# Band and stick-breaking attention: weights of B as differences, late division in A, and two more tiles turned by VectorE

## The chip, the cores and the metric

The kernel runs on one core of one Trainium2 chip. The metric is the device time of one execution in microseconds (us); the median of several executions is compared. PE is TensorE, DVE VectorE, ACT ScalarE, POOL GpSimd and SP the engine from whose queue all transfers (DMAs) of this kernel are issued. Each engine works off its instructions in the order in which they were written into its queue.

## What is computed

One layer of a hybrid encoder, for 1024 prompt frames and for 32 sample frames with a cache of 512. Width 1024; two groups of 8 heads of 64, A and B. All in float32.

```python
qa, ka, va, ga, qb, kb, vb, gb = split(rmsnorm(h, g_pre) @ w_in)

def band_attention(q, k, v, q_pos, k_pos, bias_table):          # A
    s = q @ k.T * 64**-0.5 + bias_table[clip(k_pos - q_pos, -128, 128) + 128]
    ok = same chunk of 64 frames, or one of the 8 chunks before
    return softmax(where(ok, s, -1e30)) @ v

def stick_breaking(q, k, v, q_pos, k_pos):                      # B
    z = q @ k.T * 64**-0.5
    causal = k_pos < q_pos
    log_1m = where(causal, log_sigmoid(-z), 0.0)
    after = cumsum(log_1m, reverse=True) - log_1m               # over later keys
    w = where(causal, exp(log_sigmoid(z) + after), 0.0)
    return w @ v

y = concat(oA * silu(ga), oB * silu(gb)) @ w_out
h = h + rmsnorm(y, g_post)
h = h + sigmoid(h @ w_ple_gate) * (p @ w_ple)
```

In words, a weight of B is sigmoid(z) of its key times the product of sigmoid(-z) over all later keys up to the query.

## The kernel before

**Stages.** The input is normalised and turned so that the model width lies on the partitions. A projection of 128 columns of `w_in` (`col_steps`) is 3 chunks of 352 frames with 24 products each. The eight pairs of heads come in the order A0, B0, A1, B1, A2, B2, A3, B3; while the attention of one pair runs, the projections k, q and v of the next are computed, and beside the last pair the eight gate projections (`mm_gA`, `mm_gB`). Then follow the output projection (`o`), the second norm and the last gate (`g`), with a Strassen-like scheme of seven products.

**Products in parts.** A float32 operand is split into an upper half `hi` (rounded to fp32r, a copy) and a lower half `lo` (the difference), and products are summed over the halves. So every operand that PE reads costs a copy, mostly on ACT, and a subtraction, on DVE or POOL.

**Attention of a head** (`attention`). Eight tiles i of 128 queries. A tile of A reads the key blocks from max(0, i - 4) to i, a tile of B the blocks from 0 to i, so tiles of B grow from 1 to 8 blocks (36 a head), those of A to 5 (30 a head).

- `scores(i)`: PE puts the scores into one or two PSUM banks (`SA`, `SB`; tag S, three banks). For A, DVE adds the bias (`biasA`) and takes the running maximum in one operation (`tensor_tensor_reduce`, in the profile CUSTOM_DVE_ANT_0), negates the maximum, ACT takes the exponential with the sum, DVE the reciprocal, POOL scales. For B, DVE masks the diagonal block, ACT takes sigmoid(-z) into `w0` and sigmoid(z) into `w1`, DVE runs the product from the last key backwards (`tensor_tensor_scan`, shifted by one column), and POOL multiplies the two.
- `weights_t(i)`: the weights are turned so that keys lie on the partitions. In general PE does it block by block (`ptwA`, `ptwB`), ACT takes the upper half from PSUM into `wTh`, DVE the lower half into `wTl`. Tiles in `ROUND` go another way: DVE turns 32x32 squares from `w1` into `w0` (STREAM_TRANSPOSE), one DMA stores the result (`swapA`), four load it back into `w1` with the blocks in their places, and the halves are taken from there. Before the change these are tiles 4 and 6 of A.
- `values(g)`: for each half g of the head's queries one accumulation of `wT` with the values (`PVA`, `PVB`) and a sum of two row groups, stored in `o_dr`.

Tiles 4 and 6 have 5 blocks each in A, 5 and 7 in B.

**Rooms.** `w0` and `w1` of a tile lie in two rings of columns (`Arena`: `om` with 3076, `be` with 3384 columns), `wTh` and `wTl` in rings of 33 blocks. A room in a ring is given out in order, and taken again only when its last reader is done. A head of B takes 13 blocks for its first half and 29 for its second; one of A 13 and 20.

**Order.** All instructions are first recorded (`Recorder`) with their dependences. A planner (`order`) then runs a list schedule with a cost for each operation, a margin for landing transfers and a rule for the access path that DVE and POOL share, and the kernel is written in the order that comes out. On PE, attention has precedence over the projections wherever it is ready. Any change to an operation's engine or size therefore changes the order of much else.

**Gates.** A gate chunk loads its part of the head output (`og`), takes the sigmoid on ACT, and multiplies on DVE and POOL. All recorded operations have the one source line 450 in the profile; tiles are told apart by name.

## Time and profile before

| | |
|---|---|
| median of 3 runs | 806.25 us |
| the runs | 804.82, 806.25, 810.35 us |
| span of the profiled execution (first to last instruction) | 802.6 us |
| its busy time: PE, DVE, ACT, POOL | 792.0, 565.7, 539.5, 469.5 us |
| moved by DMA | 146.32 MB, 182 GB/s |

The execution that was profiled has no time of its own beside its span; the median stands 3.65 us above the span. A line of a group gives engine, operation, what is written and read by the program's names, partitions x elements, the number of instructions, then busy time, mean ns of one, idle time of the engine just before them and what ended it. A group without a single shape mixes several ("+3 forms"). A busy time of PE counts overlapping records once. In a timeline the columns are start, duration, engine, operation; in the chain of waits start and length of a piece of the chain. A row of the stages gives the stretch, its length, and for PE, the weight loads (PEld), DVE, ACT and POOL the busy time and number of instructions, then granted clock, DMA share and GB/s. SPq is the queue from which transfers are issued.

### The profile page before, as it was taken

The page shows a single profiled execution, that of the slowest core. Times are in us where ns is not written, and L with a number is a line of the kernel's source. Part 1 is how long each engine was busy: PE and PEld are TensorE (multiplying, and loading weights), DVE is VectorE, ACT ScalarE, POOL GpSimd, SP SyncE. Part 2 cuts the span into 40 slices and gives each one's busy share as a digit, 9 for nine tenths or more (in the row PEclk, how much of TensorE's full clock was granted, in tenths as well). Part 3 has the DMA queues.
Part 4 walks back from the last instruction along what each step waited for, and adds up shares of the span by engine and source line. Part 5 has one row for each costly group of instructions (what it writes and reads, how often), then busy time and mean ns, then how long its engine had stood idle before and what let it go on. Part 6 is the DMA issues. An engine that isn't in the chain of part 4 may idle for free.

```text
span 802.6 us, 14554 instructions
## 1 busy us (share of the span) xinstructions
PE 792.0 (99%) x4734; PEld 731.4 (91%) x4734; DVE 565.7 (70%) x1129; ACT 539.5 (67%) x1163; POOL 469.5 (58%) x554
## 2 busy tenths in 40 slices
PE   9999999999999999999999999999999999999997
PEld 7899999999999999999999899999998877888786
DVE  7627878777787888776787586854554786587655
ACT  6636787786586777776787577644437868876741
POOL 6625867795686866635473265554553448599613
PEclk9999999999999999999999999999999999999999
DMA  9419986538876565833325656344389957769634
GB/s 293 135 46 285 236 230 186 153 112 254 220 229 198 145 184 158 208 103 102 92 60 141 146 158 205 99 149 138 105 277 300 288 174 242 236 197 345 215 117 131
DMA packets 147390, 146.32 MB, mean 182 GB/s; under 512 B 37409, under 2 KB 109257, under 8 KB 147314
## 3 DMA queue, kind: packets, MB, share of 16 engines
q1 hardware_dynamic: 147314, 145.39, 61.3%
q8 instruction: 38, 0.62, 0.3%
q14 instruction: 38, 0.31, 0.1%
HBM read 90.78 MB, written 46.16 MB: 171 GB/s over the span
## 4 chain that ended last, share of the span: by engine, by line
PE 89%; DVE 3%; DMA 2%; POOL 2%; ACT 1%; issue 1%; SPq 1%; POOLq 0%; DVEq 0%; ACTq 0%
PE mm_gB L450 6%; PE mm_gA L450 6%; PE mm_kB L450 6%; PE mm_qB L450 6%; PE mm_qA L450 5%; PE mm_kA L450 5%; PE mm_vB L450 4%; PE PVB L450 4%; PE mm_vA L450 4%; PE SB L450 4%; PE ptwB L450 4%; PE SA L450 3%; PE PVA L450 3%; PE g0P L450 2%; PE g1P L450 2%; PE o1P L450 2%
## 5 line engine op out<-in xcount | busy, mean ns | idle before, releaser
L450 POOL TENSOR_TENSOR be<-be,om 128x512 f32<-128x512 f32 (+8 forms) x66 | 82.9, 1260 | 77.8 <-DVE om L450 43.9
L450 DVE TENSOR_TENSOR_SCAN om<-om,SB 128x384 f32<-128x384 f32 (+5 forms) x96 | 92.6, 968 | 21.9 <-ACT be L450 11.7
L450 POOL TENSOR_SCALAR be<-be,statA 128x640 f32<-128x640 f32 (+3 forms) x64 | 44.4, 698 | 44.4 <-DVE statA L450 35.8
L450 DVE TENSOR_TENSOR wTl<-ptwB,wTh 128x512 fp32r<-128x512 f32 (+3 forms) x96 | 50.8, 546 | 13.8 <-ACT wTh L450 12.4
L450 ACT ACTIVATE om<-SB 128x384 f32<-128x384 f32 (+5 forms) x96 | 47.4, 499 | 19.0 <-DVE SB L450 14.2
L450 ACT CAST wTh<-ptwB 128x512 fp32r<-128x512 f32 (+3 forms) x96 | 44.6, 483 | 14.5 <-PE ptwB L450 10.5
L450 ACT ACTIVATE be<-om,statA 128x640 f32<-128x640 f32 (+3 forms) x64 | 44.6, 698 | 11.2 <-DVE statA L450 9.6
L450 ACT ACTIVATE be<-SB 128x384 f32<-128x384 f32 (+5 forms) x96 | 46.8, 498 | 6.8 <-DVE om L450 6.3
L450 PE MATMUL ptwB<-ident,be 128*128 128x128 f32 x288 | 44.0, 273 | 0.1
L450 PEld LDWEIGHTS ptwB<-ident,be 128*128 128x128 f32 x288 | 34.9, 140 | 2.2 <-PE mm_vA L450 0.4
L450 DVE CUSTOM_DVE_ANT_0 om<-SA,biasA 128x320 f32<-128x320 f32 (+2 forms) x64 | 30.7, 480 | 5.3 <-PE SA L450 4.9
L450 PE MATMUL SB<-kdB,LB 128*128 128x384 f32 (+5 forms) x96 | 34.0, 357 | 0.3 <-DVE om L450 0.3
L450 ACT CAST wTh<-ptwA 128x512 fp32r<-128x512 f32 (+2 forms) x64 | 26.0, 429 | 12.0 <-PE ptwA L450 11.4
L450 DVE TENSOR_TENSOR wTl<-ptwA,wTh 128x512 fp32r<-128x512 f32 (+2 forms) x64 | 29.7, 482 | 4.9 <-ACT wTh L450 4.0
L450 PE MATMUL SB<-klB,LB 128*128 128x384 f32 (+5 forms) x96 | 32.9, 347 | 0.0
L450 PE MATMUL SA<-kdA,LA 128*128 128x320 f32 (+2 forms) x96 | 30.0, 319 | 1.1 <-DVE LA L450 0.8
L450 PE MATMUL SA<-klA,LA 128*128 128x320 f32 (+2 forms) x96 | 29.8, 319 | 0.0
L450 POOL TENSOR_TENSOR gB<-gB,gB 128x256 f32<-128x256 f32 x32 | 26.6, 848 | 0.7 <-DMA gB<-in_w_ple_gate_dram 0.4
L450 PE MATMUL ptwA<-ident,be 128*128 128x128 f32 x160 | 26.5, 274 | 0.0
L450 DVE TENSOR_TENSOR SB<-SB,maskb 128x128 f32<-128x128 f32 x64 | 18.0, 292 | 9.9 <-PE SB L450 8.0
L450 POOL TENSOR_TENSOR oB<-oB,oB 128x256 f32<-128x256 f32 x32 | 23.6, 754 | 1.4 <-DMA oB<-in_w_out_dram 1.3
L450 POOL TENSOR_TENSOR h<-h,x 128x512 f32<-128x512 f32 (+1 forms) x18 | 23.0, 1295 | 0.8 <-DVE h L450 0.8
(706 smaller groups left out, 2668.3 us busy)
## 6 DMA issues: line engine op xcount, KB each, us to landing
swapA<-om SPq DMA_DIRECT2D x16, 320.0 KB, 3.5
be<-swapA SPq DMA_DIRECT2D x64, 80.0 KB, 2.9
oB<-in_w_out_dram SPq DMA_DIRECT2D x16, 256.0 KB, 3.9
sum_dro<-oB SPq DMA_DIRECT2D x16, 256.0 KB, 2.9
gB<-in_w_ple_gate_dram SPq DMA_DIRECT2D x16, 256.0 KB, 3.7
sum_drg<-gB SPq DMA_DIRECT2D x16, 256.0 KB, 3.2
x<-in_x_prompt_dram SPq DMA_DIRECT2D x16, 256.0 KB, 4.1
h_dr<-h SPq DMA_DIRECT2D x8, 512.0 KB, 3.6
```

The costliest lines, as they stand in the source:

```text
L450: getattr(getattr(tc.nc, o.what[0]), o.what[1])(*args, **kw)
```

## The change

- **Differences for B.** The scan is no longer shifted: it runs in place over sigmoid(-z), so that `w0` holds the running products P, with a 1 behind the last key. The weight is P of the next key less P of its own, since sigmoid(z) = 1 - sigmoid(-z). The second sigmoid goes, and POOL's product becomes a subtraction. The sample heads of B keep the old way.
- **Late division for A.** The exponentials stay unscaled. Their sums are kept for the whole head; behind the last tile they are inverted together, turned by PE and stored in `rs_dr`. A gate chunk of A loads them spread over 64 partitions, and POOL multiplies once more. The sample columns of `rs_dr` are filled with ones.
- **Signs.** Queries of A, the bias and the mask are negated, so the reduction takes a minimum and the exponential a scale of -1; the negation of the maximum goes.
- **Turned tiles.** Tiles 4 and 6 of B are turned by DVE squares and DMAs too. The lower halves of all such tiles are subtracted by POOL in place of DVE.
- **Rooms.** The ring `be` shrinks to 3328 columns; `og` moves from the tag `bias` (2 deep) to `stg` (3 deep).

```diff
@@ -28,7 +28,7 @@
 
 
 
-ROUND = {"A": ((4,),(6,)), "B": ()}
+ROUND = {"A": ((4,),(6,)), "B": ((4,),(6,))}
 LAG_T = 2
 LAG_V = 2
 SPACE_S = 0.1
@@ -477,6 +477,7 @@
         return Buf(shape, F32, name=name, real=dram.tile(shape, F32, tag=name, name=name))
 
     o_dr = [scratch([P, T], f"o_dr{n}") for n in range(8)]
+    rs_dr = scratch([8, T], "rs_dr")
     og_dr = scratch([8, P, T], "og_dr")
     h1_dr = scratch([T, D], "h1_dr")
     sum_dr = {w: scratch([4, 4, P, 512], f"sum_dr{w}") for w in "og"}
@@ -511,7 +512,7 @@
     at0 = rec.pool(ctx, tc, name="at0", bufs=1)
     at = rec.pool(at_stack, tc, name="at", bufs=1)
     opnd = [at0, at]
-    ring0, ring1 = Arena(rec, at, "om", 3076), Arena(rec, at, "be", 3384)
+    ring0, ring1 = Arena(rec, at, "om", 3076), Arena(rec, at, "be", 3328)
     ringh, ringl = (Arena(rec, at, x, 33 * P, F32R) for x in ("wTh", "wTl"))
 
     def rstd_of(ms, name, n):
@@ -524,6 +525,11 @@
 
 
     NAMES = ["qA", "kA", "vA", "gA", "qB", "kB", "vB", "gB"]
+
+    def fixed_columns():
+        x = small.tile([8, NS], F32, tag="fixed", name="fixed")
+        nc.gpsimd.memset(x, 1.0)
+        dma(rs_dr[:, SEQ:T], x)
 
     raws, loaded = {}, {}
 
@@ -609,8 +615,8 @@
         dma(rb, rel_bias[0])
         R = ring1.tile([8, 768], "R")
         nc.gpsimd.memset(R, 0.0)
-        nc.vector.tensor_scalar(R[:, 256:768], R[:, 256:768], rb[:, 0:1], None, ALU.add)
-        nc.vector.tensor_copy(R[:, 0:256], rb[:, 0:256][:, ::-1])
+        nc.vector.tensor_scalar(R[:, 256:768], R[:, 256:768], rb[:, 0:1], None, ALU.subtract)
+        nc.vector.tensor_scalar(R[:, 0:256], rb[:, 0:256][:, ::-1], -1.0, None, ALU.mult)
         dma(r_dr, R)
 
     def bias_src(h, rows, first, cols):
@@ -728,8 +734,12 @@
             acc = box["acc"]
             cs = slice(c * CH, (c + 1) * CH)
             if k == "g" and part == 0:
-                box["og"] = at2.tile([P, CH], F32, tag="bias", name=f"og{kind}{p}_{c}", bufs=2)
-                dma(box["og"], o_dr[n][:, cs])
+                box["og"] = at2.tile([P, 2, CH], F32, tag="stg", name=f"og{kind}{p}_{c}", bufs=3)
+                dma(box["og"][:, 0], o_dr[n][:, cs])
+                if ab == "A":
+                    for h in range(2):
+                        row = rs_dr.real[2 * p + h:2 * p + h + 1, cs]
+                        dma(box["og"][h * HD:(h + 1) * HD, 1], Raw(rs_dr, bass.AP(tensor=row.tensor, offset=row.offset, ap=[[0, HD], [1, CH]])))
             W = loaded[j]
             for x in range(part * 24 // PARTS, (part + 1) * 24 // PARTS):
                 q, k8 = x // KD, x % KD
@@ -742,10 +752,12 @@
                 sg = at2.tile([P, 512], F32, tag="sg", name=f"sg{kind}{p}_{c}", bufs=3)[:, 0:CH]
                 nc.scalar.activation(sg, acc, AF.Sigmoid)
                 nc.vector.tensor_tensor(sg, acc, sg, ALU.mult)
-                nc.gpsimd.tensor_tensor(sg, sg, box["og"], ALU.mult)
+                nc.gpsimd.tensor_tensor(sg, sg, box["og"][:, 0], ALU.mult)
+                if ab == "A":
+                    nc.gpsimd.tensor_tensor(sg, sg, box["og"][:, 1], ALU.mult)
                 dma(og_dr[n, :, cs], sg)
             elif k == "q":
-                nc.scalar.activation(box["st"][:, cs], acc, AF.Copy, scale=SCALE)
+                nc.scalar.activation(box["st"][:, cs], acc, AF.Copy, scale=-SCALE if ab == "A" else SCALE)
             else:
                 nc.scalar.copy(box["st"][:, cs], acc)
 
@@ -785,9 +797,10 @@
             if ab == "A":
                 bias = at2.tile([P, 640], F32, tag="bias", name=f"bias{nm}", bufs=2)
                 dma(bias, bias_src(2 * p + h, P, 0, 640))
-                nc.gpsimd.memset(bias[0:HD, 0:HD], NEG)
-                nc.gpsimd.memset(bias[HD:P, 576:640], NEG)
+                nc.gpsimd.memset(bias[0:HD, 0:HD], -NEG)
+                nc.gpsimd.memset(bias[HD:P, 576:640], -NEG)
                 box["bias"] = bias
+                box["sums"] = small.tile([P, 8], F32, tag="sums", name=f"sums{nm}", bufs=2)
 
         def lo_block(i):
             return max(0, i - 4) if ab == "A" else 0
@@ -832,23 +845,26 @@
                 nc.gpsimd.memset(w0[:, n:n + 1], 1.0)
                 for a, b, s in pieces:
                     nc.scalar.activation(w0[:, a:b], s, AF.Sigmoid, scale=-1.0)
-                for a, b, s in pieces:
-                    nc.scalar.activation(w1[:, a:b], s, AF.Sigmoid)
                 for a, b, s in reversed(pieces):
-                    rev = w0[:, a + 1:b + 1][:, ::-1]
-                    nc.vector.tensor_tensor_scan(rev, rev, s, 1.0 if b == n else w0[:, b + 1:b + 2], ALU.mult, ALU.bypass)
-                nc.gpsimd.tensor_tensor(w1[:, 0:n], w1[:, 0:n], w0[:, 1:n + 1], ALU.mult)
+                    rev = w0[:, a:b][:, ::-1]
+                    nc.vector.tensor_tensor_scan(rev, rev, s, w0[:, b:b + 1], ALU.mult, ALU.bypass)
+                nc.gpsimd.tensor_tensor(w1[:, 0:n], w0[:, 1:n + 1], w0[:, 0:n], ALU.subtract)
             else:
                 m = small.tile([P, 4], F32, tag="stat", name=f"stat{nm}_{i}", bufs=6)
+                sums = box["sums"]
                 for j, (a, b, s) in enumerate(pieces):
                     nc.vector.tensor_tensor_reduce(
                         w0[:, a:b], s, box["bias"][:, n - b:n - a][:, ::-1], 1.0,
-                        -3e38 if j == 0 else m[:, j - 1:j], ALU.add, ALU.max, m[:, j:j + 1])
+                        3e38 if j == 0 else m[:, j - 1:j], ALU.add, ALU.min, m[:, j:j + 1])
                 last = len(pieces) - 1
-                nc.vector.tensor_scalar(m[:, 2:3], m[:, last:last + 1], -1.0, None, ALU.mult)
-                nc.scalar.activation(w1[:, 0:n], w0[:, 0:n], AF.Exp, bias=m[:, 2:3], accum_out=m[:, 3:4])
-                nc.vector.reciprocal(m[:, 3:4], m[:, 3:4])
-                nc.gpsimd.tensor_scalar(w1[:, 0:n], w1[:, 0:n], m[:, 3:4], 1.0, ALU.mult, ALU.mult)
+                nc.scalar.activation(w1[:, 0:n], w0[:, 0:n], AF.Exp, bias=m[:, last:last + 1], scale=-1.0, accum_out=sums[:, i:i + 1])
+                if i == 7:
+                    nc.vector.reciprocal(sums, sums)
+                    pt = psum("T", f"pts{nm}")
+                    nc.tensor.transpose(pt[0:8, 0:P], sums, ident)
+                    row = at.tile([P, 4 * P], F32, tag="ot", name=f"sumrow{nm}", bufs=2)[0:8, 0:P]
+                    nc.scalar.copy(row, pt[0:8, 0:P])
+                    dma(rs_dr[2 * p + h, 0:SEQ].rearrange("(i q) -> i q", q=P), row)
             state[i] = w0, w1
 
         wT = {}
@@ -890,7 +906,7 @@
                     src = turned[:, :, first[x]:first[x] + cost(x), :]
                     hi, lo = (y.rearrange("p (b g q) -> p g b q", g=4, q=32) for y in (hi, lo))
                     nc.scalar.copy(hi, src)
-                    nc.vector.tensor_tensor(lo, src, f(hi), ALU.subtract)
+                    nc.gpsimd.tensor_tensor(lo, src, f(hi), ALU.subtract)
                 done_with.clear()
                 return
             for b in range(0, n, 4):
...
@@ -1382,6 +1397,7 @@
         dma(*x)
         rec.behind()
     bias_rows()
+    fixed_columns()
     for h in range(4):
         dma(masks[h * NS:(h + 1) * NS, :], maskb[0:NS, 0:NS])
     for j in range(3):
```

In the sample heads of A (left out) the same three signs change.

More of the change, by code (lines that the diff above doesn't have):

```diff
@@ L1017, in scores @@
                         w0[:, a0:b0], s, bx["bias"][:, NK - b0:NK - a0][:, ::-1], 1.0,
-                        -3e38 if j == 0 else m[:, 0:1], ALU.add, ALU.max, m[:, j:j + 1])
-                nc.vector.tensor_scalar(m[:, 2:3], m[:, 1:2], -1.0, None, ALU.mult)
-                nc.scalar.activation(w1[:, 0:NK], w0[:, 0:NK], AF.Exp, bias=m[:, 2:3], accum_out=m[:, 3:4])
+                        3e38 if j == 0 else m[:, 0:1], ALU.add, ALU.min, m[:, j:j + 1])
+                nc.scalar.activation(w1[:, 0:NK], w0[:, 0:NK], AF.Exp, bias=m[:, 1:2], scale=-1.0, accum_out=m[:, 3:4])
                 nc.vector.reciprocal(m[:, 3:4], m[:, 3:4])
```

## The prediction

> **What bounds the kernel now.** I read the page first (parts 1, 2, 4, 5), then the groups by shape, the chain of waits in one stretch, the stages, and the timelines of a B head.
>
> ```profile
> PE 792.0 (99%) x4734; PEld 731.4 (91%) x4734; DVE 565.7 (70%) x1129; ACT 539.5 (67%) x1163; POOL 469.5 (58%) x554
> PEclk9999999999999999999999999999999999999999
> PE 89%; DVE 3%; DMA 2%; POOL 2%; ACT 1%; issue 1%; SPq 1%; POOLq 0%; DVEq 0%; ACTq 0%
> L450 POOL TENSOR_SCALAR be<-be,statA 128x640 f32<-128x640 f32 (+3 forms) x64 | 44.4, 698 | 44.4 <-DVE statA L450 35.8
> L450 ACT CAST wTh<-ptwB 128x512 fp32r<-128x512 f32 (+3 forms) x96 | 44.6, 483 | 14.5 <-PE ptwB L450 10.5
> L450 ACT ACTIVATE be<-SB 128x384 f32<-128x384 f32 (+5 forms) x96 | 46.8, 498 | 6.8 <-DVE om L450 6.3
> L450 PE MATMUL ptwB<-ident,be 128*128 128x128 f32 x288 | 44.0, 273 | 0.1
> ```
>
> PE is busy in 792.0 of 802.6 us at full granted clock and carries 89% of the chain. So work taken from PE shortens the run, provided PE still always has something ready; work on DVE, ACT and POOL counts only through the waits it makes. The 288 turnings of B's weights are PE work that the change cuts by a third: blocks of tiles 4 and 6 are 5 + 7 = 12 of 36 a head, over 8 heads 96. A busy PE is pipelined, so the worth of one turning is read from the chain, where pieces don't overlap:
>
> ```profile
> 300.63 0.77 PE ptwB L450 x7
> 306.81 0.87 PE ptwB L450 x8
> ```
>
> Seven take 0.77 us, eight 0.87: 0.110 us each, not the 273 ns of the record.
>
> **The change part by part.** *PE.* 96 x 0.110 = 10.6 us go. The sums of A's late division add one turning a head of 8, at most 0.110 each (it is a smaller one): 0.9 us come. Net -9.7 us. Nothing else on PE changes.
>
> *DVE.* The rows:
>
> ```profile
> L450 DVE TENSOR_TENSOR wTl<-ptwB,wTh 128x512 fp32r<-128x512 f32 x48 | 32.4, 681 | 12.1 <-ACT wTh L450 11.1 <-PE PVB L450 0.6
> L450 DVE TENSOR_TENSOR wTl<-ptwB,wTh 128x384 fp32r<-128x384 f32 x16 | 8.7, 543 | 0.0
> L450 DVE TENSOR_TENSOR wTl<-ptwB,wTh 128x128 fp32r<-128x128 f32 x16 | 4.5, 279 | 0.2
> L450 DVE TENSOR_TENSOR wTl<-be,wTh 128x640 fp32r<-128x640 f32 x16 | 18.1, 1131 | 4.6 <-ACT wTh L450 4.2
> L450 DVE STREAM_TRANSPOSE om<-be 128x640 f32<-128x640 f32 x16 | 13.4, 838 | 3.1 <-POOL be L450 3.1
> L450 DVE RECIPROCAL statA<-statA 128x1 f32<-128x1 f32 x64 | 9.7, 155 | 3.8 <-ACT be L450 3.3
> L450 DVE TENSOR_SCALAR statA<-statA 128x1 f32<-128x1 f32 x64 | 9.5, 149 | 1.2
> ```
>
> Tiles 4 and 6 of B had four lower halves a head, 681 + 279 + 681 + 543 ns, 17.5 us over 8 heads. A's lower halves, 18.1 us, go to POOL; 64 negations (9.5) go; of 64 reciprocals 8 stay (-8.5). Added are squares for 640 + 896 columns a head at 838/640 = 1.31 ns: 16.1 us. Net -37.5 us.
>
> *ACT.* The second sigmoid goes: -46.8 us. The upper halves of the 96 blocks, a third of 44.6, are replaced by copies from SBUF whose price is near (the first row below: 727/640 x 12,288 columns = 14.0 against 14.9). Net about -47 us.
>
> *POOL.* A's scaling goes, -44.4 us. The lower halves come: A 16 x 640 and B 12,288, together 22,528 columns.
>
> ```profile
> L450 ACT CAST wTh<-be 128x640 fp32r<-128x640 f32 x16 | 11.6, 727 | 0.7 <-DMA be<-swapA 0.6
> L450 POOL TENSOR_TENSOR be<-be,om 128x640 f32<-128x640 f32 x8 | 10.6, 1319 | 11.0 <-DVE om L450 5.3 <-ACT wTh L450 4.4 <-PE PVA L450 1.3
> L450 POOL TENSOR_TENSOR wl_gB<-wr_gB,wh_gB 128x512 fp32r<-128x512 f32 x8 | 10.5, 1318 | 5.4 <-ACT wh_gB L450 3.6 <-DMA og_dr<-sggA 1.8
> L450 POOL TENSOR_TENSOR sggA<-sggA,oggA 128x352 f32<-128x352 f32 x12 | 11.5, 960 | 11.0 <-DVE sggA L450 9.7 <-issue 1.3
> ```
>
> POOL has no lower half of the turned, strided form. Bounds are 2.06 ns a column (1319/640) and 2.57 (1318/512, the same subtraction into fp32r); I take 2.57, 58 us, since it is the same operation. With 12 more products in gates A (11.5 us) POOL gains 25 us and stands near 495 us, far under PE. B's product becomes a difference of the same shape: no change. [...]
>
> *DMA.* Each of 16 new turned tiles adds a store and four loads, together 12.6 MB; 24 spreads of A's sums (2.2 MB), 8 stores of them and one fill come on top, some 113 issues on SP. Bytes grow by 10% of 146.32. Nothing of this is on PE, but the weights of tiles 4 and 6 now reach PE by way of SP, whose queue is in order:
>
> ```profile
> 192.46 0.85 DVE L450 STREAM_TRANSPOSE om<-be 128x640 f32<-128x640 f32 x1 [0.93 <-POOL be L450]
> 193.33 0.33 SPq L450 DMA_DIRECT2D swapA<-om  x1
> 211.33 0.67 SPq L450 DMA_DIRECT2D be<-swapA  x1
> 216.52 0.72 ACT L450 CAST wTh<-be 128x640 fp32r<-128x640 f32 x1
> 233.05 0.82 DVE L450 STREAM_TRANSPOSE om<-be 128x640 f32<-128x640 f32 x1
> 244.88 0.73 ACT L450 CAST wTh<-be 128x640 fp32r<-128x640 f32 x1
> ```
>
> From squares to upper half A's round trip takes 11.8 us when SP is free and 24.1 when the last load stands 18 us behind the store. Behind a waiting load stand the weight loads of the projections; behind a lower half waiting on POOL stand the one-column MEMSET that the scan of the next tile now reads, and DVE behind that scan. With 1.0 for ACT and POOL's 2.3 (896 x 2.57) the trip of tile 6 is 15 to 27 us.
>
> Who needs it: the product PV of a head's second half, which in B comes soon after tile 6 is ready (POOL's 128x896), in head 0 and head 1 of the second B pair:
>
> ```profile
> 262.39 1.77 POOL L450 TENSOR_TENSOR be<-be,om 128x896 f32<-128x896 f32 x1 [2.86 <-DVE om L450]
> 276.33 1.17 PE L450 MATMUL PVB<-wTh,v2B 128*128 128x512 f32 x4
> 298.48 1.77 POOL L450 TENSOR_TENSOR be<-be,om 128x896 f32<-128x896 f32 x1 [0.91 <-DVE om L450]
> 308.46 1.09 PE L450 MATMUL PVB<-wTh,v2B 128*128 128x512 f32 x4
> ```
>
> 12.2 and 8.2 us from the end of one to the start of the other. So PV comes 3 to 19 us later, and with it the next head's turning, since the wT rings hold 33 blocks and a B head's two groups need 13 + 29. PE's cover is the projection of the next pair. It is thin at the end of a B pair: the next-but-one projection starts (302.20) before the key tile that it needs is even read out by POOL (301.06 + 2.40), so it is as early as it can be. After an A pair 24.5 us are left (338.87 to 363.40). In the last B pair the gates cover: 29.26 us of them stand alone at its end.
>
> ```profile
> 301.06 2.40 POOL L450 TENSOR_TENSOR klA<-stkA,kdA 64x1024 fp32r<-64x1024 f32 x1
> 302.20 1.46 PE L450 MATMUL mm_kB<-hnh,wh_kB 128*128 128x352 f32 x8
> 336.47 2.40 POOL L450 TENSOR_TENSOR klB<-stkB,kdB 64x1024 fp32r<-64x1024 f32 x1 [1.37 <-ACT kdB L450]
> 363.40 1.46 PE L450 MATMUL mm_kA<-hnh,wh_kA 128*128 128x352 f32 x8
> 576.32 29.26 PE mm_gB L450 x181
> ```
>
> Against that delay B's chain gets shorter: each piece of scores leaves its PSUM bank 0.5 us earlier (no second sigmoid, row of 498 ns), and DVE and ACT each lose some 40 us. In the stage of that pair the side engines already have air:
>
> ```profile
> 224.00:298.00 74.00, 73.80 (x487) 70.78 (x486) 59.96 (x107) 57.42 (x134) 52.92 (x69) 1.00 0.67 192
> ```
>
> DVE 59.96, ACT 57.42, POOL 52.92 of 74. I therefore take the two as nearly cancelling and charge 0.9 us of new PE waits, between 0 and the saving itself.
>
> *At no cost:* the negated scores and bias, the fill and the small tiles (few, early). The gates' operand moves to a three-deep ring shared with the later `php` tiles, which now wait for gate B; two gate chunks (24 products each, 29.26/181 = 0.162 us a product, 3.9 us a chunk) follow the one that frees the first, and hide the copy; uncovered, 2 us.
>
> *Sum.* 802.6 - 9.7 + 0.9 = 793.8 us of span. The median of the runs, 806.25, lies 3.65 over the profiled span, for start and end, which don't change: **797.4 us**.
>
> **The rivals.** *B's chain doesn't let the saving out (chance 0.27).* If at the ends of the second and third B pairs attention, not PE, sets the pace, what PE saves there turns into idle time: half of 10.6, 5.3 us, is kept, less 0.9: 801.9 us. For it speaks 302.20 against 303.46 above; against it PE's 73.80 of 74.
>
> *The round trip becomes the bound (0.22, slower).* PV of B's second half late by the middle of 3 and 19, 11 us, in the four heads of those two pairs; one projection chunk of 3.9 us still fits into the free PSUM bank, so 7.1 x 4 = 28 us of PE waits: 797.4 - 0.9 + 28 = 825 us. That is without help from the shorter chain; with it (12 pieces of scores a head, 0.5 us each) it decides from a trip of 22 us on: 10.2, the mean of 12.2 and 8.2, and 3.9, 6 and 8.8/4 for the saving. For it: the 24.1 us above, and SP's 113 more issues. Against it: A's trips, long ones too, cost PE nothing so far; these are PE's longest wait and the only one for turned weights:
>
> ```profile
> PE idle L450 <- DVE newh L450: 1.3, 1, 1.3
> PE PVA L450 <- ACT wTh L450: 0.2, 1, 0.2
> ```
>
>
> *Each turning is worth its whole record (0.02).* 88 x 0.273 = 24 us: 782 us. The chain's 0.110 speaks against it. [...]
>
> [...]
>
> **How the numbers follow.** My forecast has 0.46, by itself between 792 (no new wait, and some of the 10.6 us that PE idles today gone) and 800. A measurement of this kernel tells about 1%, 8 us, from no change: faster is under 798.2, slower over 814.3. Faster: nearly all of my case (0.44) and the small rival below it, 0.46. Same: its rest, the uncashed saving and POOL, 0.32. Slower: 0.22, the round trip. The range from 791 reaches up to 815, halfway into the late round trip; beyond it some 0.14 lies above and 0.03 below.
>
> **What would show it.** Turnings ptwB x192, PE busy near 782, ACT near 492, DVE near 528, POOL near 495. Right: PE's share stays at 99% in the B stages. Wrong: PE idle before PVB or SB there, put down to wTl from POOL or to swapB loads; or a PE that is as busy as before with 96 turnings less.

## The result and the profile after

The changed kernel takes 815.89 us in the median of four runs (814.96 to 818.86), beside 805.77 us for the kernel before on the same chip: ratio 1.0108, 95% interval [1.0075, 1.014]. It is slower by 1.1%, on the other side of the forecast of 797.4 us, and 0.9 us outside the range. Single executions of the kernel before, here and beside the experiments, lie between 804.8 and 811.4 us, but for one of 966 us at a granted clock of 0.753 that no ratio counts; so a difference of 2 or 3 us between two medians is no evidence by itself. The profiled execution of the changed kernel took 818.86 us, 2.2 us over its span of 816.7 us. Its page, busy times by engine, granted clock in 40 slices, and the chain by engine:

```profile
PE 790.8 (97%) x4646; PEld 725.0 (89%) x4646; DVE 544.1 (67%) x975; ACT 508.6 (62%) x1065; POOL 479.1 (59%) x535
PEclk9999999999999999999999999999999899999999
PE 77%; ACT 5%; POOL 5%; issue 4%; DVE 4%; DMA 4%; SPq 1%; POOLq 0%; ACTq 0%; DVEq 0%
```

PE has 88 products less and is nevertheless busy for 790.8 us, 1.2 less than before; and it idles 816.7 - 790.8 = 25.9 us where it idled 10.6. PE's part of the chain falls from 89% to 77%. DVE and ACT have less to do, POOL 2% more, and the run is 14.1 us longer. The groups that the change touched (busy, mean ns | idle before and its releaser):

```profile
L450 POOL TENSOR_TENSOR wTl<-be,wTh 128x640 fp32r<-128x640 f32 x24 | 38.6, 1609 | 31.8 <-ACT wTh L450 31.8
L450 POOL TENSOR_TENSOR wTl<-be,wTh 128x896 fp32r<-128x896 f32 x8 | 17.7, 2208 | 1.4 <-ACT wTh L450 1.4
L450 ACT CAST wTh<-be 128x640 fp32r<-128x640 f32 (+1 forms) x32 | 24.9, 780 | 6.7 <-DMA be<-swapA 6.6
L450 PE MATMUL ptwB<-ident,be 128*128 128x128 f32 x192 | 29.3, 273 | 0.5 <-POOL be L450 0.5
L450 ACT ACT_TABLE_LOAD x14 | 18.0, 1283 | 1.5 <-PEq L1855 0.7 <-DVE SB L450 0.4
```

192 turnings are there as foretold, and POOL's lower half costs 1609/640 = 2.51 and 2208/896 = 2.46 ns a column, close to the 2.57 that was taken. Two things are new. POOL's queue stands still for 33 us in all in front of its lower halves, waiting for ACT's upper half. And ACT loads its tables 14 times; the kernel before has x8, 10.3 us.

PE's waits, in total, times, and longest (some of the rows):

```profile
PE PVA L450 <- ACT wTh L450: 2.5, 2, 1.4
PE o1P L450 <- ACT oB L450: 2.4, 1, 2.4
PE ptwA L450 <- ACT be L450: 2.3, 3, 1.0
PE SB L450 <- DVE om L450: 2.0, 4, 1.2
...
PE PVB L450 <- DVE wTl L450: 0.3, 1, 0.3
```

There is no one wait that took the saving: many of one or two microseconds are spread over attention, projections and output, for as many releasers. PVB, where the second rival put its 28 us, waits for 0.3. The stages of 100 us, before first, then after (stretch, length, then PE, PEld, DVE, ACT, POOL, granted clock, DMA share, GB/s):

```profile
200.00:300.00 100.00, 99.68 (x655) 96.05 (x654) 81.17 (x167) 72.46 (x168) 70.12 (x92) 1.00 0.70 196
300.00:400.00 100.00, 100.00 (x650) 97.05 (x650) 76.02 (x174) 74.73 (x163) 54.44 (x70) 1.00 0.52 135
400.00:500.00 100.00, 98.99 (x643) 95.22 (x643) 75.25 (x182) 71.99 (x159) 49.44 (x58) 1.00 0.51 138
600.00:700.00 100.00, 100.00 (x464) 80.58 (x463) 63.59 (x102) 79.16 (x163) 52.62 (x52) 1.00 0.78 253
```

```profile
200.00:300.00 100.00, 93.30 (x588) 87.71 (x587) 71.44 (x134) 64.30 (x145) 61.57 (x84) 0.98 0.69 191
300.00:400.00 100.00, 98.15 (x632) 94.28 (x631) 74.20 (x142) 69.09 (x144) 61.01 (x67) 1.00 0.69 187
400.00:500.00 100.00, 96.77 (x623) 92.38 (x623) 71.20 (x146) 69.20 (x152) 48.47 (x46) 1.00 0.53 144
600.00:700.00 100.00, 96.40 (x436) 77.16 (x434) 65.79 (x106) 71.34 (x148) 44.69 (x47) 0.97 0.77 249
```

The largest loss is between 200 and 300 us: 6.4 us of PE. ACT, DVE and POOL are each less busy there too, so on the average of the stage none of them has become full. The chain of waits inside it:

```profile
212.32 5.61 DMA be<-in_cache_a_v_dram
...
217.94 5.03 DMA be<-swapA
...
223.07 0.73 ACT wTh L450
...
223.93 1.58 POOL wTl L450
...
226.40 0.90 PE ptwA L450 x3
```

A turned tile of A comes back from its round trip at 222.97. ACT takes the upper half, POOL the lower; only then does ACT write the next tile's exponentials into the ring `be` (its wait is put down to `wTl`), and PE turns them. Every piece is one that the prediction knew. The rows of PE at that place (idle time before a group, and its releaser, in brackets):

```profile
221.39 1.30 PE L450 MATMUL mm_vB<-hnh,wh_vB 128*128 128x352 f32 x7
223.85 0.85 PE L450 MATMUL PVA<-wTh,v2A 128*128 128x512 f32 x4 [1.16 <-ACT wTh L450]
224.53 0.37 PE L450 MATMUL mm_vB<-hnh,wh_vB 128*128 128x352 f32 x1
224.74 0.64 PE L450 MATMUL mm_vB<-hnh,wl_vB 128*128 128x352 f32 x3
226.40 0.90 PE L450 MATMUL ptwA<-ident,be 128*128 128x128 f32 x3 [1.02 <-ACT be L450]
...
230.86 1.01 PE L450 MATMUL mm_vB<-hnh,wl_vB 128*128 128x352 f32 x5
```

PE had not run out of projection. The chunk of `mm_vB` that begins at 221.39 has 24 products; 7 of them are done before the first gap and 17 after it, and they need the same weights that the chunk before it had used by 221.6. These 17 were ready, but they stand behind `PVA` and `ptwA` in PE's queue. The same holds 11 to 15 us later: PE waits 0.40 us before an `SB` at 237.54 and 0.84 us before a `ptwA` at 241.29, with products of the next chunk, also begun, behind them. So 3.4 of the 6.7 us that PE idles from 200 to 300 us are waits at the head of its queue with ready work behind. The planner had put the attention product first because it took its operands to be ready by then.

The clock falls here too, as stretches of one microsecond show (columns as above):

```profile
222.00:223.00 1.00, 0.69 (x5) 0.39 (x3) 0.41 (x1) 0.00 (x0) 0.00 (x0) 1.00 0.21 68
223.00:224.00 1.00, 0.15 (x1) 0.15 (x2) 0.00 (x0) 0.93 (x2) 0.07 (x1) 1.00 0.76 295
225.00:226.00 1.00, 0.39 (x3) 0.10 (x1) 0.00 (x0) 0.47 (x1) 1.00 (x2) 0.91 0.00 0
226.00:227.00 1.00, 0.60 (x4) 0.60 (x4) 0.02 (x1) 0.95 (x4) 0.98 (x5) 0.50 0.00 0
227.00:228.00 1.00, 1.00 (x5) 0.90 (x4) 0.96 (x4) 0.00 (x0) 0.00 (x0) 0.50 0.29 109
228.00:229.00 1.00, 1.00 (x5) 0.90 (x4) 0.07 (x2) 0.00 (x0) 0.00 (x0) 0.50 0.92 258
229.00:230.00 1.00, 1.00 (x8) 0.96 (x8) 0.00 (x0) 0.00 (x0) 0.00 (x0) 0.88 0.47 156
```

From about 225.8 to 229.2, 3.4 us, PE's granted clock is 0.50, after 4 us, from 222 to 226, of which PE was busy for 2.2. A second stretch at 0.50, from 632.0 to 638.8 us, is twice as long; it begins among PE's gaps in the output projection. The mean granted clock of the run is 0.993; before it was 0.999.

**Busy times clock.** PE's busy time times its mean granted clock estimates its work at full clock. For the kernels of this study, from their profiles (the one with the last B pair alone turned by PE lies between the two kinds, with 787.6 and 23.9):

| kernels | products of PE | PE busy x clock, us | PE idle, us |
|---|---|---|---|
| before | 4734 | 791.2 | 10.6 |
| eight more in which B is turned by PE | 4734 or 4742 | 790.6 to 795.0 | 10.8 to 19.3 |
| after | 4646 | 785.3 | 25.9 |
| nine more in which B's tiles 4 and 6 are turned by squares, in every B pair | 4638 or 4646 | 781.7 to 786.4 | 19.9 to 38.0 |

The means of the two kinds are 792.4 and 783.5: the 96 turnings took 8.9 us with them, near the 9.7 that were predicted net. So the saving came, on the mean of the kinds; between the two kernels of the prediction it is 5.9. After against before, 785.3 - 791.2 = -5.9 us of work stand against +15.3 us of idling and +4.7 us of lower clock (790.8 x 0.007 less 792.0 x 0.001): together the 14.1 us of the spans. The ranges of PE's idle time don't overlap: the least of any version with squares, 19.9 us, is above the most of any version without, 19.3. The question of the experiments is where the idling comes from.

### The profile page after: what moved, and what is told of

The parts are those of the page before. It is cut to its first block, busy times and chain, and to the rows that moved or that the text cites. A ratio compares the mean times of both kernels' runs of the same rounds, so it can differ in the third digit from the quotient of the medians.

```text
span 816.7 us, 14272 instructions
## 1 busy us (share of the span) xinstructions
PE 790.8 (97%) x4646; PEld 725.0 (89%) x4646; DVE 544.1 (67%) x975; ACT 508.6 (62%) x1065; POOL 479.1 (59%) x535
## 4 chain that ended last, share of the span: by engine, by line
PE 77%; ACT 5%; POOL 5%; issue 4%; DVE 4%; DMA 4%; SPq 1%; POOLq 0%; ACTq 0%; DVEq 0%
PE mm_gB L450 6%; PE mm_gA L450 6%; PE mm_qA L450 5%; PE mm_kA L450 5%; PE mm_qB L450 4%; PE mm_kB L450 4%; PE mm_vA L450 4%; PE PVB L450 4%; PE SB L450 3%; PE o0P L450 3%; PE PVA L450 3%; PE mm_vB L450 2%; PE SA L450 2%; PE g0P L450 2%; PE g1P L450 2%
## 5 line engine op out<-in xcount | busy, mean ns | idle before, releaser
L450 POOL TENSOR_TENSOR be<-om 128x128 f32<-128x128 f32 (+6 forms) x64 | 74.3, 1170 | 38.4 <-DVE om L450 20.2
L450 POOL TENSOR_TENSOR wTl<-be,wTh 128x640 fp32r<-128x640 f32 (+1 forms) x32 | 56.3, 1758 | 33.2 <-ACT wTh L450 33.2
L450 ACT ACTIVATE be<-om,statA 128x640 f32<-128x640 f32 (+4 forms) x64 | 44.4, 695 | 12.3 <-DVE statA L450 5.9
L450 ACT CAST wTh<-ptwB 128x512 fp32r<-128x512 f32 (+3 forms) x64 | 29.4, 481 | 28.8 <-PE ptwB L450 22.2
L450 DVE CUSTOM_DVE_ANT_0 om<-SA,biasA 128x320 f32<-128x320 f32 (+3 forms) x64 | 29.8, 484 | 21.1 <-PE SA L450 7.5
L450 DVE TENSOR_TENSOR wTl<-ptwB,wTh 128x512 fp32r<-128x512 f32 (+3 forms) x64 | 34.0, 548 | 13.3 <-ACT wTh L450 8.0
L450 DVE TENSOR_TENSOR wTl<-ptwA,wTh 128x512 fp32r<-128x512 f32 (+2 forms) x64 | 29.9, 484 | 16.1 <-ACT wTh L450 15.0
L450 DVE STREAM_TRANSPOSE om<-be 128x640 f32<-128x640 f32 (+1 forms) x32 | 28.9, 903 | 4.2 <-ACT be L450 2.3
L450 ACT CAST wTh<-be 128x640 fp32r<-128x640 f32 (+1 forms) x32 | 24.9, 780 | 6.7 <-DMA be<-swapA 6.6
L450 DVE TENSOR_TENSOR SB<-SB,maskb 128x128 f32<-128x128 f32 x64 | 17.7, 291 | 17.0 <-PE SB L450 16.6
L450 POOL TENSOR_TENSOR klB<-stkB,kdB 64x1024 fp32r<-64x1024 f32 x8 | 20.0, 2506 | 13.8 <-PE PVsA L450 5.9
L450 POOL TENSOR_TENSOR sggA<-sggA,oggA 128x352 f32<-128x352 f32 x24 | 23.3, 970 | 8.0 <-DVE sggA L450 5.1
```

The source lines that it names most:

```text
L450: getattr(getattr(tc.nc, o.what[0]), o.what[1])(*args, **kw)
```

## The experiments

The expectations number the theories in the order in which they came up; the last, the order itself, was formed after the others had not added up. Ratios are to the kernel before, run beside each.

**Parts taken out of the change.** First, B's weights turned by PE again.

```diff
-ROUND = {"A": ((4,),(6,)), "B": ((4,),(6,))}
+ROUND = {"A": ((4,),(6,)), "B": ()}
```

> The changed kernel with B's tiles 4 and 6 turned by TensorE again; differences, late division and A's lower halves on GpSimd stay. Theory 1 (the round trips of B's turned tiles let PE run dry, and end attention late): PE gets 10.6 us of work back but loses its new gaps, so 802 to 807 us, with PE busy near 800 of its span and no gap above 1.5 us between 200 and 260. Rival (GpSimd's lower halves are the cost): A still has half of them, so 811 us or more, gaps before PVA. Rival (late division): 814 us or more.

Measured 813.12 us, 1.0083 [1.0056, 1.011], not the 802 to 807 of the first theory. PE idles 16.7 us and has 792.0 us of work again: 2.8 us faster than the whole change by the medians, 2.0 by the ratios, whose intervals overlap, with 96 turnings more. Next, the lower halves on VectorE:

```diff
-                    nc.gpsimd.tensor_tensor(lo, src, f(hi), ALU.subtract)
+                    nc.vector.tensor_tensor(lo, src, f(hi), ALU.subtract)
```

> The changed kernel with the lower halves of the turned tiles subtracted by VectorE again, B's tiles still turned by squares. Theory 1: 812 to 818 us, the gaps remain. Rival (GpSimd's lower halves hold its queue and come late): 800 to 807 us, and the last PVB of attention ends 10 us or more earlier than at 595.7.

Measured 807.21 us, 0.9997 [0.998, 1.0014]: the best order found with B turned by squares, level with the kernel before. Its busy times, its 200 to 300 us, and the lower halves on VectorE:

```profile
PE 784.9 (97%) x4646; PEld 722.2 (90%) x4646; DVE 576.0 (72%) x1007; ACT 508.0 (63%) x1063; POOL 437.6 (54%) x503
```

```profile
200.00:300.00 100.00, 96.79 (x624) 91.83 (x624) 79.36 (x139) 61.76 (x136) 60.63 (x83) 1.00 0.72 201
```

```profile
L450 DVE TENSOR_TENSOR wTl<-be,wTh 128x640 fp32r<-128x640 f32 x24 | 25.8, 1074 | 3.2 <-ACT wTh L450 2.9
L450 DVE TENSOR_TENSOR wTl<-be,wTh 128x896 fp32r<-128x896 f32 x8 | 10.2, 1271 | 3.0 <-ACT wTh L450 3.0
```

Half of the stage's loss is gone, and PVB ends attention at 583.0 in place of 595.7. The same subtraction takes 1074 and 1271 ns on VectorE, 1609 and 2208 on GpSimd, 1.5 and 1.7 times as much; VectorE's 128x640 form of before, 1131 ns, had 1.77 ns a column against the 2.57 taken for GpSimd, 1.45 times.

Then A divided tile by tile again; the spreads of the sums and the gates' second product go too:

```diff
-                if i == 7:
...
+                nc.vector.reciprocal(sums[:, i:i + 1], sums[:, i:i + 1])
+                nc.gpsimd.tensor_scalar(w1[:, 0:n], w1[:, 0:n], sums[:, i:i + 1], 1.0, ALU.mult, ALU.mult)
```

> The changed kernel with A's weights scaled by GpSimd in each tile again and no sums stored. Theory 1: 813 to 822 us, since GpSimd gets 44 us of work back and nothing is relieved. Rival (late division, with its turned sums and its loads in the gates, is the cost): 800 to 808 us.

Measured 814.84 us, 1.0103 [1.008, 1.0126]: as slow as the change. Undoing the late division gains nothing. Then the last B pair alone by PE:

```diff
-        together = {i: g for g in ROUND[ab] for i in g}
+        together = {i: g for g in (() if (ab, p) == ("B", 3) else ROUND[ab]) for i in g}
```

> The changed kernel with tiles 4 and 6 of the last B pair alone turned by TensorE. Theory 1, part 2 (the late end of attention delays the loads of the output projection's weights, and PE stands still at 624 to 634): the last store of B's output comes 10 us or more earlier than at 597, the output projection starts without a gap, 808 to 812 us (2.6 us more PE work, some 7 less in that stage). Rival (the gap there has another cause, DMA traffic of the gates for instance): 815 to 819 us, gap still there.

815.19 us, 1.0103 [1.0068, 1.0138]. In the change attention ends some 20 us later than before (last PVB near 595.7 against 575.9), the room of the weights of the output projection opens later (their loads begin at 600.1 against 582.9), and later in that projection PE stands still:

```profile
628.00:630.00 2.00, 1.18 (x6) 0.63 (x4) 0.48 (x1) 0.62 (x1) 0.00 (x0) 1.00 0.93 289
630.00:632.00 2.00, 0.44 (x1) 0.19 (x1) 0.46 (x1) 0.96 (x2) 1.27 (x1) 1.00 1.04 399
632.00:634.00 2.00, 1.27 (x3) 0.50 (x2) 1.40 (x3) 2.00 (x5) 0.00 (x0) 0.50 1.03 346
```

That gap is gone with this edit, where the loads begin at 589.1, and another of 2.5 us has opened before 746.95, in the middle of the last gate: the time is the same. That the late loads make the gap is not shown: with the lower halves on VectorE they begin at 587.9, and PE waits 2.5 us in the same projection. A gap that an edit removes isn't a gain if the edit draws all other waits anew. The first two edits together, B by PE and the lower halves (A's alone, then) on VectorE:

> Differences and late division alone: B's tiles 4 and 6 turned by TensorE, lower halves on VectorE. If GpSimd's lower halves cost A about 6 us (theory 2: they wait at the head of GpSimd's queue), this is 804 to 808 us, like the kernel before, the pair of edits being neutral for TensorE. Rival (differences or late division cost time by themselves): 811 to 815 us, like the kernel with only B's turning undone (813).

813.32 us, 1.0057 [1.0031, 1.0083], 6.1 us more by the medians (4.8 by the ratios) than the version with VectorE's lower halves and the squares. By this pair the squares of B gain 5 to 6 us; by the change and the first run above, where GpSimd has the lower halves, they cost 2 to 3, or nothing. In both pairs PE idles more with the squares: 20.6 against 16.4 us here, 25.9 against 16.7 there.

**Table loads, lower halves of A alone, planned trips.** Between exponentials and sigmoids ACT loads a table, 1.28 us each time, and with one function for both 2 of the 14 loads are left (below). In the timeline of ACT at the border between a pair of A and one of B the changed kernel goes back and forth:

```profile
235.34 1.28 ACT L450 ACT_TABLE_LOAD   x1
236.63 0.55 ACT L450 ACTIVATE om<-SB 128x128 f32<-128x128 f32 x2
237.71 0.49 ACT L450 ACTIVATE om<-SB 128x384 f32<-128x384 f32 x1 [0.53 <-DVE SB L450]
238.21 1.28 ACT L450 ACT_TABLE_LOAD   x1
239.50 0.83 ACT L450 ACTIVATE be<-om,statA 128x640 f32<-128x640 f32 x1
...
247.54 1.28 ACT L450 ACT_TABLE_LOAD   x1 [0.43 <-DVE SB L450]
```

Before there is one load at each such border; here there are three at three of them. The planner has no price for a load. The two kernels with one function for both, which then don't compute the softmax, but have every queue in the same order but for the loads:

```diff
-                nc.scalar.activation(w1[:, 0:n], w0[:, 0:n], AF.Exp, bias=m[:, last:last + 1], scale=-1.0, accum_out=sums[:, i:i + 1])
+                nc.scalar.activation(w1[:, 0:n], w0[:, 0:n], AF.Sigmoid, bias=m[:, last:last + 1], scale=-1.0, accum_out=sums[:, i:i + 1])
```

> The changed kernel with A's exponential replaced by a sigmoid, so that ScalarE never changes its table; the order of instructions stays the same one by one, and A's weights are not a softmax. Theory 3 (14 table loads of 1.28 us, six more than before, fall where TensorE runs dry): 806 to 811 us, and the gaps at 237 to 250 and 309 to 312 go. Rival (GpSimd's lower halves alone): 814 to 817 us.

> The kernel before with A's exponential replaced by a sigmoid, no change of ScalarE's table, A's weights not a softmax. In the changed kernel the same took off 7.2 us for 12 loads. If each load costs its share wherever it falls, 6 loads here give 3 to 4 us, 802 to 804 us; if only the interleaved loads at the borders cost time, 805 to 807 us.

The changed kernel with 2 loads takes 808.66 us, 1.0012 [0.9988, 1.0036], 7.2 us less than with 14; the kernel before with 2 takes 804.84, 0.9972 [0.9949, 0.9996], some 1.4 us less (by its ratio, 2.3) than with 8. The order being the same, this is the effect of the loads alone: 0.6 us for each of 12 in the one, 0.2 to 0.4 for each of 6 in the other, whose 804.84 lies between the two cases of its expectation. Of the 10 us between the two kernels, 5 to 6 are the table loads in this order.

```diff
+                    (nc.vector if ab == "A" else nc.gpsimd).tensor_tensor(lo, src, f(hi), ALU.subtract)
```

> The changed kernel with A's lower halves back on VectorE, B's on GpSimd. If A's tiles hold GpSimd's queue (their wait is the longer one: 31.8 of 33.2 us stand before the 640-column form, which A and B share), 806 to 810 us. Rival (B's tiles do): 812 to 816 us.

812.46 us, 1.0056 [1.0034, 1.0078]: with A's lower halves on VectorE and B's on GpSimd it lies between the two, as the rival had it.

The planner lets a load land a fixed margin after its transfer. The loads of turned tiles were let land 3 us later, and 1.5 us earlier:

```diff
-                done = line + DMA_MARGIN
+                done = line + DMA_MARGIN + o.extra
...
+                    rec.ops[-1].extra = 3000.0
```

> The changed kernel with the planner told that the loads of turned tiles land 3 us later, so that their halves are put further back in the queues; no instruction is added or moved to another engine. Theory 2 (the lower half waits at the head of GpSimd's queue for transfers that land later than planned, 33 us in all): the idle time before GpSimd's wTl falls below 15 us and the time to 805 to 811 us. Rival (GpSimd's longer subtraction itself, or the late end of attention): idle time falls, the time stays at 813 to 820 us.

> The changed kernel with the planner told that the loads of turned tiles land 1.5 us earlier than it assumes; the mirror of the run with 3 us more (837.1 us, 21 us worse). If the planned round trip sets the pace through the rooms of the rings (theory 1 in its wider form: each trip holds a room and the wT ring), the time falls by up to half of that, 805 to 813 us. Rival (waits at the head of the queues on late transfers, theory 2): more of them, idle time before GpSimd's wTl above 33 us and 817 us or more.

837.14 us, 1.0377 [1.0321, 1.0433], and 819.36 us, 1.0144 [1.0099, 1.0189]. Neither is faster, and POOL's standing time before its lower halves went the other way than expected both times: it rose to 41.2 us with the longer plan, where it should have fallen, and fell to 24.3 with the shorter, where the rival had it rise, while the run got no faster. So nothing here speaks for trips that the planner takes for too short, or for POOL's standing time as the cost.

**Parts done alone.** On the kernel before, only the differences for B:

```diff
-                for a, b, s in pieces:
-                    nc.scalar.activation(w1[:, a:b], s, AF.Sigmoid)
...
+                nc.gpsimd.tensor_tensor(w1[:, 0:n], w0[:, 1:n + 1], w0[:, 0:n], ALU.subtract)
```

> The kernel before with the differences for B alone. The pair of differences and late division cost 4.6 us without any TensorE work added but 0.9 us. If the differences carry it (a new order at the borders of A and B), 808 to 812 us; if late division does, 803 to 807 us, since ScalarE only loses 47 us of work.

and only the late division with the signs and the smaller ring:

> The kernel before with late division and the changed signs alone (B's weights as products with two sigmoids). If late division carries the cost of the pair (the turned sums wait on TensorE's queue, A runs into B and the tables of ScalarE change more often), 809 to 813 us; if the differences do, 804 to 808 us.

814.5 us, 1.01 [1.0064, 1.0137], and 817.51 us, 1.0147 [1.011, 1.0184]. Both lie above their ranges. Each part alone costs as much as all of them together, and the differences only take work away: ACT is busy for 506.8 us in place of 539.5. Costs of parts that don't add up to the whole, and work left out that makes the run longer, speak for something that every edit brings with it. There is one such thing: the planner's order.

**The order alone.** Two constants of the planner were moved a little, with no edit of the work: the price of a semaphore, and the margin of transfers.

```diff
-SEM = 60
+SEM = 64
```

> The kernel before with one cost of the planner, the time of a signal between engines, at 64 in place of 60 ns: the same instructions in another order, no edit of the work. Theory 4 (the order of before is a good draw for its very costs, and any edit draws a new, ordinary one): 809 to 818 us, as far off as the differences alone (814.5). Rival (orders are alike within half a per cent, and each edit costs by its own): 804 to 808 us.

```diff
-DMA_NS, DMA_RATE, DMA_MARGIN = 1500, 320.0, 2000
+DMA_NS, DMA_RATE, DMA_MARGIN = 1500, 320.0, 2050
```

> The same with the planner's margin for a transfer at 2050 in place of 2000 ns. Theory 4: 809 to 818 us. Rival: 804 to 808 us.

815.29 us, 1.0093 [1.0062, 1.0124], and 813.81 us, 1.0084 [1.0049, 1.0118]. The kernel before, with the same work in another order, loses nearly as much as the whole change does. Its page and its stage from 200 to 300 us with 64 ns:

```profile
PE 794.2 (98%) x4734; PEld 731.7 (90%) x4734; DVE 564.0 (69%) x1129; ACT 543.6 (67%) x1167; POOL 470.9 (58%) x554
```

```profile
200.00:300.00 100.00, 93.88 (x607) 89.20 (x606) 73.51 (x147) 71.29 (x158) 61.81 (x86) 1.00 0.64 184
```

The same work, and 5.8 us of PE are lost in the very stage in which the change lost 6.4. The new orders also have more table loads, 12 and 10 in place of 8; at the 0.6 us of the run above that is an estimate of 2.4 and 1.2 us of the 9.5 and 8.0, so the loads are a part of it and not the whole. The counterpart is the edit without a new order: the differences for B, where the second sigmoid stays in the plan and is left out only when the kernel is written, so that the queues of PE, DVE, POOL and SP are in the order of before, instruction by instruction, and ACT's lacks only the second sigmoids.

```diff
                     nc.scalar.activation(w1[:, a:b], s, AF.Sigmoid)
+                    rec.ops[-1].ghost = True
...
+                if o.ghost:
+                    continue
```

> The differences for B in exactly the order of the kernel before: the second sigmoid is still planned, but not written; all other instructions stand in their old places on every engine. Theory 4: the edit itself costs nothing once the order is kept, 802 to 806.5 us against 814.5 with a new order. Rival (the differences themselves are dearer, by the scan's start from memory or the subtraction): 808 us or more.

```profile
PE 792.1 (99%) x4734; PEld 732.1 (91%) x4734; DVE 570.6 (71%) x1129; ACT 504.5 (63%) x1067; POOL 465.0 (58%) x554
```

808.09 us, 1.0003 [0.9981, 1.0025], where the same edit with its own order has 1.01. The time falls into the rival's range by a hair (808 or more), but the kernel before took 806.98 beside it, and the ratio decides. ACT has 35 us less to do and PE is as busy as before: the edit is worth nothing and costs nothing; its 1% was the order, with the two table loads more that came with it.

**More orders of the change.** The changed kernel with 64 ns and with the margin of 2050, and the version with VectorE's lower halves with 64 ns:

> The changed kernel with the time of a signal at 64 ns in the planner: another draw of its order. Theory 4: it moves by several us against 815.9 in either direction, between 806 and 822. Rival (its level is set by the edits): 814 to 818 us.

> The changed kernel whole, with the planner's DMA margin at 2050 ns instead of 2000: no operation is changed, only the order that the planner writes out, a third order of the same work (815.9 and 826.4 us so far; the kernel before has given 806, 815.3 and 813.8 in three orders). Theory 4 (the order decides most of what is seen): anything from 810 to 826 us, and the three changed orders together stand some us above the three of the kernel before. Rival (the change itself costs nothing and its two orders were unlucky): under 810 us.

> The changed kernel with the lower halves of the turned tiles on VectorE (807.2 us in its first order) and the planner's semaphore price at 64 ns instead of 60: a second order of the same work; the changed kernel with 64 ns gave 826.4 us. If GpSimd's lower halves are what costs, whatever the order: 8 us or more under that, 805 to 818 us. If the 807.2 us was one lucky order: 820 to 828 us.

| planner's constants | before | after | after, lower halves on VectorE |
|---|---|---|---|
| 60 and 2000 ns | 805.8, 8 loads | 815.89, 14 loads | 807.21, 0.9997 [0.998, 1.0014], 12 loads |
| 64 and 2000 ns | 815.29, 12 loads | 826.41, 1.0238 [1.02, 1.0276], 14 loads | 815.86, 1.0109 [1.0065, 1.0152], 14 loads |
| 60 and 2050 ns | 813.81, 10 loads | 812.17, 1.0075 [1.005, 1.01], 12 loads | not run |

Loads are table loads; 826.41 lies above the range that was expected of it.

Up to the table loads, one and the same work spreads over 9.5 us before and over 14.2 us after. The means are 811.6 and 818.2 us: 6.5 us apart, less than the spread of either. In the third row the two are level (1.0084 and 1.0075). Over three orders each, that the change is slower by itself is not shown. GpSimd's lower halves cost 8.7 and 10.6 us in the two rows that have both; but 812.17 us with them, in the third order, is below 815.86 without in the second, so they too are not separated from the order for good.

No version that was run and computes the layer beats the kernel before.

## Why the prediction was wrong

**What held.** The turnings: 96 less, and PE's work less by 8.9 us, where 9.7 net were predicted from the chain's 0.110 us each, not from the record's 273 ns. POOL's price a column, 2.5 ns. The round trip in B: the trip of tile 6 from squares to the end of the lower half, forecast at 15 to 27 us, reads in the timeline of the second B pair

```profile
273.91 1.08 DVE L450 STREAM_TRANSPOSE om<-be 128x896 f32<-128x896 f32 x1
288.65 0.94 ACT L450 CAST wTh<-be 128x896 fp32r<-128x896 f32 x1
289.66 2.80 POOL L450 TENSOR_TENSOR wTl<-be,wTh 128x896 fp32r<-128x896 f32 x1 [0.27 <-ACT wTh L450]
290.17 0.81 PEld L450 LDWEIGHTS PVB<-wTh,v2B 128*128 128x128 f32 x4
292.73 0.82 PEld L450 LDWEIGHTS PVB<-wTl,v2B 128*128 128x128 f32 x4
```

18.6 us, and PE takes the product with the upper half while POOL still subtracts: no wait. Over all eight such tiles the trip takes 16.7 to 27.2 us. So the rival "the round trip becomes the bound" had neither its place nor its price, although the time came out slower; the long trip that did stop PE (the one landing at 222.97) is one of A, of which the prediction said that such trips cost PE nothing so far. The rival "B's chain doesn't let the saving out" had the kind of loss right, what PE saves turns into idle time, and not its place: of PE's larger gaps only 1.5 us (before 309.16 and 311.48) and 0.5 us (before 435.61) lie at the ends of the second and third B pairs.

**Sizes off the path.** ACT stands at 508.6 where 492 was predicted: 7.7 us of it are six table loads more, which the prediction left out of its sum, and the second sigmoids, taken at 46.8 us from their group's busy time, take only 35 off ACT's where the order is kept (539.5 to 504.5). DVE has 544.1 against 528 and POOL 479.1 against 495; in the page's 40 slices DVE is always under 90% busy, and POOL reaches 90% in three, as before. The chances name POOL beside the uncashed saving; that its work is dearer than the forecast took it, no run shows: its lower halves cost 2.51 and 2.46 ns a column, under the 2.57.

**The step that failed** is the charge for new waits: "I therefore take the two as nearly cancelling and charge 0.9 us of new PE waits, between 0 and the saving itself." It came to 15.3 us of idling and 4.7 us of lower clock. The reasoning weighed one delay (the trip) against one relief (a shorter chain in B). The trip came out as forecast, and what the shorter chain gave was not measured; what the reasoning took for granted stands in its first part, "provided PE still always has something ready". Ready work was there, as the 17 products of `mm_vB` show; but PE took what stood next in its queue, and that had not arrived (waits of 1.16 and 1.02 us there). PE's 99% were read as a property of the kernel. They are a property of one order of it: with the same work in two other orders PE idles 17.7 and 16.1 us, not 10.6. The changed kernel could not keep that order, since every removed or moved operation makes the planner write another. The planner puts an operation where its estimates of costs and landings make it ready, table loads have no cost in it, and what arrived later than estimated held the ready work behind it; whether an order comes out that suits the real times is then largely luck, as three orders of each kernel suggest. The prediction's sum had no term for a new order. That work on DVE, ACT and POOL "counts only through the waits it makes" is borne out by the differences alone: no change where the order is kept, 1% more where it is drawn anew.

"The gates cover" in the last B pair held for PE, which is busy 100% from 500 to 600 us, but attention ended 20 us later, and PE stood still in the output projection afterwards; the run without that gap was no faster.

**What is shown and what isn't.** Shown: the saving on PE arrived; another order alone costs the kernel before 0.8 to 0.9%; the differences in the old order cost nothing; the twelve table loads that one function for both saves cost 7.2 us in the order of the change. Open: whether the change is dearer than the kernel before on the average of many orders (6.5 us over three each), whether the squares bring idle time of their own, as every version with them suggests (25.4 us on the mean against 15.3), how much of it are GpSimd's lower halves, and why exactly the first order of the kernel before is that good. The whole change in the order of before wasn't tried: its added stores and loads have no place there.

## What to carry to other kernels

Where a planner writes the instruction order, give its constants a small nudge on the unchanged kernel first: if that alone moves the time by 1%, a single run of an edit can't tell the edit from its order, and neither can the edit's parts run one by one. Read an edit on the bound engine from its busy time times its granted clock, which was steady within 5 us here over orders that lay up to 30 us apart, and keep the order (leave the operation in the plan and drop it at the end) where only the edit's own cost is asked. A busy share of 99% is a statement on an order, and an argument "PE always has something else" is not enough where a queue is worked off in order: the something else must also stand in front of the product that is late.

## What the runs showed of the hardware

PE's granted clock fell from 1.00 to 0.50 inside the second of two gaps of 1.2 and 1.0 us (222.69 to 223.85 and 225.38 to 226.40), for 3.4 us, as the one-microsecond rows show (0.91, 0.50, 0.50, 0.50, 0.88); from 222 to 226 PE was busy for 0.69, 0.15, 1.00 (the row from 224 to 225 is not shown above) and 0.39 of each. Nor does the sum of idle time go with the mean clock: the kernel with the last B pair alone by PE has 23.9 us of it at a mean clock of 0.998, VectorE's lower halves with 64 ns have 25.6 at 0.990.

A table load takes 1283 ns on the mean, in the 14 of the change as in the 8 of before; in the timeline above the next activation starts at 236.63, where the load of 235.34 ends.

The planner's rule for an access path that DVE and POOL share has its counterpart in the trace of the kernel before. DVE's 16 subtractions `wTl<-be,wTh` of 128x640 take 826 ns in the median and 800 at the least. Three begin while POOL works on `klB` and take 2.49 us, as below, 1.81 and 1.51; the first two end 0.7 us after `klB`:

```profile
442.04 2.38 POOL L450 TENSOR_TENSOR klB<-stkB,kdB 64x1024 fp32r<-64x1024 f32 x1 [0.63 <-ACT kdB L450]
442.61 2.49 DVE L450 TENSOR_TENSOR wTl<-be,wTh 128x640 fp32r<-128x640 f32 x1
```

Where DVE's begins first, 0.02 us ahead at 101.23, it takes 0.83, and POOL's `wl_kA` of 128x512 takes 1.97 us, with a median of 1.30 for the eight of its kind.
